# Moving the operands of an encoder's matmuls by 32 bytes, and another order for one stage's loads

## Chip, cores and metric

One core of a Trainium2 chip. The metric is device time of one launch in microseconds, the median of the runs; a profile of one execution goes with it. The engines are named as the profile names them: PE multiplies (PEld is its weight load), DVE and ACT work elementwise, POOL and SP here mostly issue DMAs.

## What is computed

One step of a one-layer encoder on 1024 prompt frames and 64 sample frames (1088 columns in all), width 1024, everything in fp32:

```
proj = rmsnorm(x) @ w_in                      # cb, cc, ch, q, k, v, ga, gb
ya = (cb * causal_conv(cc * ch)) @ w_conv_out
yb = band_attention(q, k, v) @ w_attn_out     # own chunk and 8 chunks before, softmax
x = x + (sigmoid(ga) * ya + sigmoid(gb) * yb) @ w_out
x = x + (silu(h @ w_ff1) * (h @ w_ff3)) @ w_ff2      # h = rmsnorm(x)
return rmsnorm(x), conv states, key and value caches
```

## The kernel before

**Precision.** Every fp32 operand is split into a rounded high part and the rest (`split`, lines 125 to 129: a cast on ACT, a subtraction on DVE). A product is three matmuls: high weights by high data, high weights by the rest of the data, rest of the weights by high data.

**Stages.** In order: norm, transposes and v (lines 443 to 600); the twelve units of the input projection (`run`, matmul at line 263); gates and attention, where PE alternates between gate products (`product`, lines 330 to 332) and attention steps; the two output products ya and yb with the merge (lines 1071 to 1099); `w_out` (wo, lines 1137 to 1142); the up projections of the feed-forward part (22 more units at line 263); the down projection (line 1621).

**A unit.** `run` does a 256 by 256 block of weights by seven products instead of eight. For each of four k it issues six matmuls of 128 rows by 272 columns, always in this order (high weights `wh..`, rest `wl..`; data plane 0 is high, plane 1 is the rest; a half is 272 columns):

| place in the six | weights | data plane, half | data address mod 64 | address of the weights loaded next, mod 64 |
|---|---|---|---|---|
| 1 | high | 0, first | 0 | 0 |
| 2 | high | 0, second | 0 | 0 |
| 3 | high | 1, first | 32 | 0 |
| 4 | high | 1, second | 32 | 32 |
| 5 | rest | 0, first | 0 | 32 |
| 6 | rest | 0, second | 0 | 0 |

"Moving operand" below means the data that is streamed, "weights" the operand that PEld loads; the weights of the next matmul are loaded while the present one streams. The addresses come from the built program. They follow from three things: tiles on the right side of SBUF (pools `apool`, `mspool`, `ws`, allocated downwards from byte 229344) all begin at 32 modulo 64; an operand's planes are rows of HT+8 = 552 floats of which the first 8 are skipped (`operand`, from line 135); high weights skip 8 floats, the rest none (`pair`, from line 142). Tiles on the left side (`t1_pool`, `tpool`, `uo`) begin at 0 modulo 64 unless something small stands ahead of them: `lead1` (line 354) and `lead` (line 1105), 8 floats each, bring `t1_pool` and `tpool` to 32, `uo` has none. The shifts at line 344 place the weights of ya and yb by hand.

**The down projection** takes its weights as moving operand (`ring_of`) and `ht` tiles as weights, both at 32 modulo 64.

**The stage that the second half of the change touches.** Gate products are the entries of `GATES`; before the last three (`LAST`) the attention pools are closed and `uo` is opened in their place with `u` (operand of ya: four pieces `u_d[k]`, 128 x 2 x 1088) and `ob` (operand of yb). Attention's output `o_d` and the reciprocals of its sums `rc_d` are loaded piece by piece, multiplied (line 1060, DVE) and split into `ob` (ACT, then DVE). `gates_in` loads stored gate values, `ga` in four tiles, `gb` in one. ya multiplies by sigmoid(ga), applied in place by ACT (line 1080); DVE then takes the product out of PSUM (line 1083). PE has five PSUM buffers there (`psum2`), so it runs at most five products ahead of DVE. All these loads stand in SP's queue, and SP waits before each load for the one eight places ahead of it: eight of its loads are in flight at most. DVE and ACT work strictly in the order in which their instructions stand.

Of the kernel before, what the change touches and what calls it, by code (L numbers as in the profile page):

```python
# [8 lines left out]
F32 = mybir.dt.float32  # L9
F32R = mybir.dt.float32r  # L10
# [5 lines left out]
P = 128  # L16
# [16 lines left out]
HT = T // 2  # L33
# [5 lines left out]
ROW, STEP = HT + 8, 144  # L39
# [27 lines left out]
def encoder_kernel(ctx: ExitStack, tc: tile.TileContext, ins, outs):  # L67
    nc = tc.nc
# [6 lines left out]

    const = ctx.enter_context(tc.tile_pool(name="const", bufs=1, reuse_waits="tile"))
    dr = ctx.enter_context(tc.tile_pool(name="dr", bufs=1, space=DRAM))
    apool = ctx.enter_context(tc.tile_pool(name="apool", bufs=1, reuse_waits="tile", side="right"))
    mspool = ctx.enter_context(tc.tile_pool(name="mspool", bufs=1, reuse_waits="tile", side="right"))
    ws = ctx.enter_context(tc.tile_pool(name="ws", bufs=8, reuse_waits="tile", side="right"))  # L80
# [13 lines left out]
    u_d = dr.tile([4, P, 2, T], F32, name="u_d")  # L94
# [30 lines left out]
    def split(hi, lo, src):  # L125

        a = act.copy(hi, src)  # L127
        b = vec.tensor_tensor(lo, src, hi.bitcast(F32), op=ALU.subtract)  # L128
        return a.ins, b.ins
# [28 lines left out]
    def three_sums(pool, nm):  # L158
        return {p: operand(pool, p, f"{nm}{p}") for p in (6, 7, 5)}
# [157 lines left out]
    def next_w():  # L317
        i = used[0]
        used[0] += 1
        prep(i + 2)  # L320
        return plan[i]
# [19 lines left out]
    for m in range(0, 8, 2):  # L341
        lds = [
            {"src": ins[nm][0][:, m * P : (m + 2) * P], "w": 2 * P, "shift": shift}
            for nm, shift in (("w_conv_out", (56, 24)), ("w_attn_out", (8, 40)))
        ]
        plan += [(ld, 4, j * P) for ld in lds for j in range(2)]

# [3 lines left out]
    t1_stack = ExitStack()  # L351
    ps1 = t1_stack.enter_context(tc.tile_pool(name="ps1", bufs=1, space=PSUM, reuse_waits="tile"))
    t1_pool = t1_stack.enter_context(tc.tile_pool(name="t1_pool", bufs=1, reuse_waits="tile"))
    t1_pool.tile([P, 8], F32, name="lead1")
    t1 = three_sums(t1_pool, "xs")

    scr = t1_pool.tile([P, 10816], F32, name="scr")
# [400 lines left out]
    for n in range(len(units)):  # L758
# [21 lines left out]
        for _ in r:  # L780
            if n < 2 and si in (2 + n, 5 + n):
                i = 2 * n + si // 5
# [24 lines left out]
    def gate(i, cs):  # L807
        g, m = GATES[i]
        dst = ga_d if g == "a" else gb_d
        for c in cs:  # L810
            o, n = PIECES[c]
            ps = pmm.tile([P, 512], F32, tag="mm", name=f"g{i}_{c}")
            product(ps[:, :n], gate_w[i], xn, o, n)
            st = st_pool.tile([P, HN], F32, tag="st", name=f"gst{i}_{c}")
            act.copy(st[:, :n], ps[:, :n])
            nc.gpsimd.dma_start(dst[m * P : (m + 1) * P, o : o + n], st[:, :n])
# [188 lines left out]
    def between():  # L1005
        credit[0] += PER
        while credit[0] >= 1:
            credit[0] -= 1
            next(steps, None)
# [3 lines left out]
    def gates_in(nm, m):  # L1013
        if nm == "gb":
            t = mp.tile([P, T], F32, tag="rc", name=f"gb{m}", bufs=3)
            nc.sync.dma_start(t, gb_d[m * P : (m + 1) * P])
            for o, n in PIECES:
                sg[nm, m, o] = t[:, o : o + n]
            return
        for o, n in PIECES:  # L1020
            t = sg[nm, m, o] = mp.tile([P, HN], F32, tag=nm, name=f"{nm}{m}_{o}", bufs=8)
            nc.sync.dma_start(t, ga_d[m * P : (m + 1) * P, o : o + n])
# [11 lines left out]
    for i in range(4, len(GATES)):  # L1034
        gate_w[i] = next_w()
        if i == len(GATES) - LAST:
            for _ in steps:
                pass
            att_stack.close()
            uo = pg_stack.enter_context(tc.tile_pool(name="uo", bufs=1, reuse_waits="tile"))  # L1040
            u, ob = (
                Acts(
                    uo.tile([P, 2, 4 * T + 8], F32R, name=nm)[:, :, : 4 * T].rearrange("p l (k t) -> p l k t", k=4)
                )
                for nm in ("u", "ob")
            )
            mp = pg_stack.enter_context(tc.tile_pool(name="mgp", bufs=4, reuse_waits="tile"))
            gates_in("ga", 0)
            for k in range(4):
                nc.sync.dma_start(u.t[:, :, k].bitcast(F32), u_d[k])  # L1050
            for k in range(4):
                o = ob.t[:, 0, k].bitcast(F32)
                nc.sync.dma_start(o, o_d[k * P : (k + 1) * P])
                r = mp.tile([P, T], F32, tag="rc", name=f"rc{k}", bufs=3)
                for j in range(2):
                    src = rc_d[2 * k + j]
                    ld = nc.sync.dma_start(
                        r[j * HD : (j + 1) * HD], bass.AP(tensor=src.tensor, offset=src.offset, ap=[[0, HD], [1, T]])
                    )
                vec.tensor_tensor(r, o, r, op=ALU.mult)  # L1060
                split(ob.t[:, 0, k], ob.t[:, 1, k], r)
            with tc.issue_after(ld.ins):
                gates_in("ga", 1)
                gates_in("gb", 0)
        for c in range(4):
            gate(i, (c,))
            between()
# [5 lines left out]
    for m0 in range(0, 8, 2):  # L1073
        for m in (m0, m0 + 1):
# [3 lines left out]
            for o, n in PIECES:  # L1078
                t = sg["ga", m, o]
# [4 lines left out]
        for m in (m0, m0 + 1):  # L1084
# [3 lines left out]
            for o, n in PIECES:  # L1088
                t, z = sg.pop(("ga", m, o)), sg.pop(("gb", m, o))
# [11 lines left out]

    hp0 = ctx.enter_context(tc.tile_pool(name="hp0", bufs=1, reuse_waits="tile"))
    early = ctx.enter_context(tc.tile_pool(name="early", bufs=1, reuse_waits="tile"))
    lead = ctx.enter_context(tc.tile_pool(name="lead", bufs=1, reuse_waits="tile"))
    lead.tile([P, 8], F32, name="lead")
    tpool = ctx.enter_context(tc.tile_pool(name="tpool", bufs=1, reuse_waits="tile"))
    up_stack = ExitStack()
    psA = up_stack.enter_context(tc.tile_pool(name="psA", bufs=2, space=PSUM, reuse_waits="tile"))
# [196 lines left out]
    def hidden_done(p):  # L1305
# [4 lines left out]
        def keep(c, x):  # L1310
            if p == NF // 2 - 1 and c in LATE:
                hq = ring_of(LATE[c])[:, 3072:4096].rearrange("p (i l t) -> p i l t", i=4, l=2)
            else:
                hq = hp.tile([P, 4, 2, P], F32R, tag="hq", name=f"hq{p}_{c}", bufs=3)
            split(hq[:, :, 0], hq[:, :, 1], x[:, :512].rearrange("p (i t) -> p i t", t=P))
            stored[0] = nc.gpsimd.dma_start(h_d[p, c - 1], hq.rearrange("p i l t -> p (i l t)").bitcast(F32)).ins  # L1316
# [45 lines left out]
    ring = {}  # L1362

    def ring_of(p):
        if p not in ring:
            pool = apool if p in (1, 2, 4, 3) else tpool
            ring[p] = pool.tile([P, 8 * ROW], F32R, tag=f"o{p}", name=f"ring{p}")[:, : 8 * HT]
        return ring[p]

    hts, loaded = [], [0]  # L1370
# [1 line left out]
    def h_load(ks, g, p):  # L1372
        ht = []
        for kp in ks:
            t = ws.tile([P, 4 * STEP], F32R, tag=("wh", "wl")[loaded[0] % 2], name=f"ht{kp}_{g}_{p}")
            t = t[:, :512].rearrange("p (i l t) -> p i l t", i=2, l=2)
            loaded[0] += 1
            nc.sync.dma_start(
                t.rearrange("p i l t -> p (i l t)").bitcast(F32), h_d[kp, p - 1, :, g * 512 : (g + 1) * 512]
            )  # L1380
            ht.append(t)
        hts.append(ht)
# [3 lines left out]
    def refill():  # L1386

        while len(hts) < len(loads_h) and held[0] + len(loads_h[len(hts)][0]) <= 16:
            held[0] += len(loads_h[len(hts)][0])
            h_load(*loads_h[len(hts)])  # L1390
# [6 lines left out]
    class Down:  # L1397
# [10 lines left out]
        def new(self, p):  # L1408
            at = self.kp % 4 * 1024
            self.w[p] = ring_of(p)[:, at : at + 1024].rearrange("p (l n) -> p l n", l=2)  # L1410
            return self.w[p][:, 0], self.w[p][:, 1]
# [99 lines left out]
    for n in range(1, len(names)):  # L1511
# [8 lines left out]
        if n in (4, 6):  # L1520
            nm, src = (("k", ck), ("v", cvv))[n // 2 - 2]
# [21 lines left out]
    bufs = {(hp, "hs"): 1, (hp, "snap"): 3, (hp, "sa"): 4, (hp0, "snap"): 1, (hp0, "sa"): 1}  # L1543
    for n, (i, d) in enumerate(order):
        if n < len(homes):
            pool, tag = homes[n]
# [27 lines left out]
    q = 0  # L1574
    for b, ks in enumerate(blocks):
        first, final = b == 0, b == len(blocks) - 1
        nk = blocks[b + 1] if not final else []
        for g in range(2):
# [28 lines left out]
            for si, js in turns:  # L1607
                p, ht = STEPS[si], hts[base + si]
                key = {1: "A", 6: "A", 5: "A", 3: "A", 2: "B", 7: "D", 4: "D"}[p]
                for j in js:  # L1610
                    i = 2 * g + j
                    if (key, j) not in ps:
                        ps[key, j] = psD.tile(
                            [P, 512], F32, tag="A" if key == "A" else "BD", name=f"{key}{b}_{i}",
                            bufs=2 if key == "A" else 4,
                        )
                    t = ps[key, j]
# [11 lines left out]
                    o = acc[i + 4 * h, d]  # L1629
# [78 lines left out]
```

## Time and profile before

| | |
|---|---|
| median of 3 runs | 1492.48 us (1492.09 to 1495.37) |
| profiled execution, its own time | 1494.22 us |
| its span, first to last instruction | 1492.3 us |
| granted TensorE clock | 0.998 |
| PE busy | 1474.8 us, 99% of the span, 10200 matmuls |
| PEld busy | 1384.6 us, 93% |
| DVE, ACT, POOL busy | 981.5, 680.4 and 129.9 us |

The profiled execution's time is 1.9 us more than its span, and 1.74 us more than the median. A matmul's duration in the profile (about 288 ns for 272 columns) is not what it costs: matmuls overlap, and what counts is the time from one start to the next.

### The profile page before, as it was taken

Reading aid. Unit: us, or ns where it says so; the run is one execution under the profiler, and the core shown is the slowest. Engines: PE = TensorE matmul, PEld = TensorE weight load, DVE = VectorE, ACT = ScalarE, POOL = GpSimd, SP = SyncE. Lnnn points to the kernel's source line nnn. Section 1 sums busy time; section 2 is a strip of 40 time slices with the busy share of each in tenths; the row PEclk is TensorE's granted clock in tenths of the full one; section 3 lists DMA queues with packets and bytes.
Section 4 is the critical chain, followed back from the end, with each engine's and each line's share of the span. In section 5 each row is a group of like instructions: output and inputs, shape, how many; then the busy total and the mean of one; then the engine's idle time right before and its main releaser. Section 6 shows DMA issues by size and latency. Waiting matters only on the chain.

```text
span 1492.3 us, 26460 instructions
## 1 busy us (share of the span) xinstructions
PE 1474.8 (99%) x10200; PEld 1384.6 (93%) x10200; DVE 981.5 (66%) x1852; ACT 680.4 (46%) x1398; POOL 129.9 (9%) x238
## 2 busy tenths in 40 slices
PE   9999999999999999999999999999999999999997
PEld 6899999999999999998889999999999999888886
DVE  7975465633777753763489767666666667857576
ACT  7654333434776652631356444444444445412123
POOL 1300010001111121000100111110011111000000
PEclk9999999999999999999999999999999999999999
DMA  8686523178676539633433454433344438777675
GB/s 287 181 271 213 175 87 116 58 211 227 189 190 179 147 109 292 201 125 130 150 113 107 145 179 161 157 134 113 118 160 145 159 133 301 265 236 239 227 261 204
DMA packets 163933, 264.72 MB, mean 177 GB/s; under 512 B 18528, under 2 KB 98592, under 8 KB 163776
## 3 DMA queue, kind: packets, MB, share of 16 engines
q1 hardware_dynamic: 143024, 196.13, 42.1%
q0 software_dynamic: 19632, 64.81, 12.0%
q10 hardware_dynamic: 1152, 2.10, 0.4%
q8 instruction: 80, 1.31, 0.4%
q14 instruction: 45, 0.37, 0.1%
HBM read 172.89 MB, written 91.92 MB: 177 GB/s over the span
## 4 chain that ended last, share of the span: by engine, by line
PE 89%; DMA 5%; DVE 3%; ACT 1%; SPq 1%; issue 1%; DVEq 0%; ACTq 0%
PE Ab L263 9%; PE Aa L263 9%; PE A L1621 8%; PE Db L263 4%; PE Da L263 4%; PE D L1621 4%; PE Bb L263 2%; PE Ba L263 2%; PE B L1621 2%; PE wo L1138 2%; PE wo L1137 2%; PE wo L1139 2%; PE t L954 2%; PE Ak L263 2%; PE Acb L263 2%; PE Ach L263 2%
## 5 line engine op out<-in xcount | busy, mean ns | idle before, releaser
L1621 PE MATMUL A<-ring,ht 128*128 128x512 f32 x528 | 124.0, 389 | 0.0
L1621 PEld LDWEIGHTS A<-ring,ht 128*128 128x128 f32 x528 | 99.1, 188 | 20.6
L330 PE MATMUL g<-xn,whp 128*128 128x272 f32 x384 | 113.1, 294 | 0.0
L331 PE MATMUL g<-xn,whp 128*128 128x272 f32 x384 | 111.7, 291 | 0.0
L332 PE MATMUL g<-xn,wlp 128*128 128x272 f32 x384 | 110.7, 288 | 0.0
L127 ACT CAST ring<-w2r 128x512 fp32r<-128x512 f32 (+1 forms) x78 | 42.6, 587 | 89.0 <-PE A L1621 50.3
L127 ACT CAST hq<-sa 128x512 fp32r<-128x512 f32 x73 | 45.2, 619 | 81.1 <-DVE sa L1332 55.8
L865 DVE CUSTOM_DVE_ANT_0 p<-s,bb 128x640 f32<-128x640 f32 (+5 forms) x72 | 47.5, 661 | 42.7 <-DMA ga_d<-gst 26.8
L1316 POOL DMA_DIRECT2D h_d<-hq x73 | 38.9, 533 | 408.7 <-DVE hq L128 218.1
L330 PEld LDWEIGHTS g<-xn,whp 128*128 128x128 f32 x384 | 72.3, 188 | 1.0
L332 PEld LDWEIGHTS g<-xn,wlp 128*128 128x128 f32 x384 | 72.4, 189 | 0.5
L331 PEld LDWEIGHTS g<-xn,whp 128*128 128x128 f32 x384 | 72.4, 188 | 0.3
L128 DVE TENSOR_TENSOR hq<-sa,hq 128x512 fp32r<-128x512 f32 x73 | 50.3, 690 | 30.1 <-ACT hq L127 29.9
L128 DVE TENSOR_TENSOR wla<-rawa,wha 128x512 fp32r<-128x512 f32 x56 | 38.4, 688 | 40.1 <-ACT wha L127 40.1
L1621 PE MATMUL D<-ring,ht 128*128 128x512 f32 x264 | 62.6, 389 | 0.0
L263 PE MATMUL Aa<-tt,wha 128*128 128x272 f32 x352 | 58.6, 288 | 0.8 <-ACT sa_Q L251 0.8
L1621 PEld LDWEIGHTS D<-ring,ht 128*128 128x128 f32 x264 | 49.6, 188 | 10.3
L263 PE MATMUL Aa<-mg,wha 128*128 128x272 f32 x352 | 58.6, 288 | 0.4 <-DVE sa L1297 0.4
L263 PE MATMUL Ab<-mg,whb 128*128 128x272 f32 x352 | 58.8, 288 | 0.0
L263 PE MATMUL Ab<-tt,whb 128*128 128x272 f32 x352 | 58.6, 288 | 0.0
L127 ACT CAST wha<-rawa 128x512 fp32r<-128x512 f32 x56 | 34.6, 620 | 52.0 <-PE Ab L263 35.5
L128 DVE TENSOR_TENSOR ring<-w2r,ring 128x512 fp32r<-128x512 f32 (+1 forms) x78 | 48.6, 645 | 11.5 <-ACT ring L127 11.5
(537 smaller groups left out, 4380.0 us busy)
## 6 DMA issues: line engine op xcount, KB each, us to landing
ht<-h_d SPq DMA_DIRECT2D x154, 256.0 KB, 3.7
h_d<-hq POOLq DMA_DIRECT2D x73, 512.0 KB, 3.4
rawa<-in_w_ff SPq DMA_DIRECT2D x11, 1024.0 KB, 5.7
rawb<-in_w_ff SPq DMA_DIRECT2D x11, 1024.0 KB, 5.3
w2r<-in_w_ff SPq DMA_DIRECT2D x11, 1024.0 KB, 7.3
qd<-q_d SPq DMA_DIRECT2D x32, 272.0 KB, 4.6
rawp<-in_w_in SPq DMA_DIRECT2D x6, 1024.0 KB, 7.0
u_d<-scr SPq DMA_DIRECT2D x8, 544.0 KB, 4.9
```

The costliest lines, as they stand in the source:

```text
L127: a = act.copy(hi, src)
L128: b = vec.tensor_tensor(lo, src, hi.bitcast(F32), op=ALU.subtract)
L263: newest[0] = mm(t[:, j, :HN], w[:, k, :], x[p][:, k, l, j * HN : (j + 1) * HN], start=p in (1, 2, 7) and k == 0 and n == 0, stop=k == 3 a ...
L330: mm(out, a, first, start=k == 0, stop=False)
L331: mm(out, a, then, start=False, stop=False)
L332: mm(out, b, p, start=False, stop=k == kt - 1)
L865: vec.tensor_tensor_reduce(out=s if len(ps.shape) == 2 else s.rearrange("p (a b) -> p a b", a=2), in0=ps, in1=bias if len(ps.shape) == 2 e ...
L954: nc.tensor.transpose(tp[:, i * P : (i + 1) * P], s[:, i * P : (i + 1) * P], ident)
L1137: mm(ps, x(k, 0), wh, start=f, stop=False)
L1138: mm(ps, x(k, 0), wl, start=False, stop=False)
L1316: stored[0] = nc.gpsimd.dma_start(h_d[p, c - 1], hq.rearrange("p i l t -> p (i l t)").bitcast(F32)).ins
L1621: mm(t, ht[k][:, j, x], w[:, l], start=p in (1, 2, 7) and k == 0 and n == 0, stop=k == len(ks) - 1 and n == 2, skip_group_check=p in (6, 5 ...
```

## The change

Part one moves addresses. A small tile `edge` (8 floats) is put at the right end of SBUF, so that everything on the right side moves 32 bytes down; `lead1` and `lead` go, so that `t1_pool` and `tpool` move with it; `uo` gets a `lead`, and the shifts of ya's and yb's weights are set anew, so that these move 32 bytes up modulo 64 together. Distances between a moving operand and the weights beside it stay, modulo 256. `ring` and `ht`, the down projection's operands, are cut 8 floats later, which puts them where they were. In the table above every 0 becomes 32 and every 32 becomes 0. Attention's operands stay.

Part two changes the order of loads. `u`'s pieces 0 and 1 stay ahead of attention's pieces 0 and 1, pieces 2 and 3 go behind the third; the four tiles of the first `ga` go from the front to behind all of them.

```diff
+    edge = ctx.enter_context(tc.tile_pool(name="edge", bufs=1, reuse_waits="tile", side="right"))
+    edge.tile([P, 8], F32, name="edge")
     apool = ctx.enter_context(tc.tile_pool(name="apool", bufs=1, reuse_waits="tile", side="right"))
...
-            for nm, shift in (("w_conv_out", (56, 24)), ("w_attn_out", (8, 40)))
+            for nm, shift in (("w_conv_out", (8, 40)), ("w_attn_out", (24, 56)))
...
-    t1_pool.tile([P, 8], F32, name="lead1")
...
+            uo.tile([P, 8], F32, name="lead")
...
-            gates_in("ga", 0)
             for k in range(4):
-                nc.sync.dma_start(u.t[:, :, k].bitcast(F32), u_d[k])
-            for k in range(4):
+                for q in {0: (0,), 1: (1,), 2: (), 3: (2, 3)}[k]:
+                    nc.sync.dma_start(u.t[:, :, q].bitcast(F32), u_d[q])
                 o = ob.t[:, 0, k].bitcast(F32)
...
             with tc.issue_after(ld.ins):
+                gates_in("ga", 0)
                 gates_in("ga", 1)
...
-    lead = ctx.enter_context(tc.tile_pool(name="lead", bufs=1, reuse_waits="tile"))
-    lead.tile([P, 8], F32, name="lead")
...
-            ring[p] = pool.tile([P, 8 * ROW], F32R, tag=f"o{p}", name=f"ring{p}")[:, : 8 * HT]
+            ring[p] = pool.tile([P, 8 * ROW], F32R, tag=f"o{p}", name=f"ring{p}")[:, 8 : 8 + 8 * HT]
...
-            t = t[:, :512].rearrange("p (i l t) -> p i l t", i=2, l=2)
+            t = t[:, 8:520].rearrange("p (i l t) -> p i l t", i=2, l=2)
```

On PE the order is the same, instruction for instruction. It differs on SP, DVE and ACT, in this stage alone (lines of the changed kernel are one or two higher). First SP's queue from the end of attention on, before:

```order
L890 DMA o_d<-co_s 64x32 x2
L1022 DMA ga_0_6566<-ga_d 128x272
L1022 DMA ga_272_6568<-ga_d 128x272
L1022 DMA ga_544_6570<-ga_d 128x272
L1022 DMA ga_816_6572<-ga_d 128x272
L1050 DMA u<-u_d 128x2x1088 x4
L1053 DMA ob<-o_d 128x1088
L1057 DMA rc_6579<-rc_d 64x1088 x2
L1053 DMA ob<-o_d 128x1088
L1057 DMA rc_6586<-rc_d 64x1088 x2
```

The same place in SP's queue of the changed kernel:

```order
L891 DMA o_d<-co_s 64x32 x2
L1052 DMA u<-u_d 128x2x1088
L1054 DMA ob<-o_d 128x1088
L1058 DMA rc_6572<-rc_d 64x1088 x2
L1052 DMA u<-u_d 128x2x1088
L1054 DMA ob<-o_d 128x1088
L1058 DMA rc_6580<-rc_d 64x1088 x2
L1054 DMA ob<-o_d 128x1088
L1058 DMA rc_6587<-rc_d 64x1088 x2
L1052 DMA u<-u_d 128x2x1088 x2
L1054 DMA ob<-o_d 128x1088
L1058 DMA rc_6596<-rc_d 64x1088 x2
```

All four pieces of `u` stood ahead of attention's first piece; now two of them stand behind nine loads of attention's pieces, and the tiles of `ga` follow at the end. On DVE, where ya's products begin to be taken out of PSUM (`ga<-ya`), before:

```order
L1060 TENSOR_TENSOR rc_6586<-ob,rc_6586 128x1088
L128 TENSOR_TENSOR ob<-rc_6586,ob 128x1088
L1083 TENSOR_TENSOR ga_0_6566<-ya_0_6979,ga_0_6566 128x272
L1060 TENSOR_TENSOR rc_6593<-ob,rc_6593 128x1088
L1083 TENSOR_TENSOR ga_272_6568<-ya_272_6994,ga_272_6568 128x272
L1083 TENSOR_TENSOR ga_544_6570<-ya_544_7009,ga_544_6570 128x272
L128 TENSOR_TENSOR ob<-rc_6593,ob 128x1088
L1083 TENSOR_TENSOR ga_816_6572<-ya_816_7024,ga_816_6572 128x272
L1060 TENSOR_TENSOR rc_6600<-ob,rc_6600 128x1088
```

And in the changed kernel:

```order
L1061 TENSOR_TENSOR rc_6580<-ob,rc_6580 128x1088
L130 TENSOR_TENSOR ob<-rc_6580,ob 128x1088
L1061 TENSOR_TENSOR rc_6587<-ob,rc_6587 128x1088
L130 TENSOR_TENSOR ob<-rc_6587,ob 128x1088
L1061 TENSOR_TENSOR rc_6596<-ob,rc_6596 128x1088
L1085 TENSOR_TENSOR ga_0_6602<-ya_0_6983,ga_0_6602 128x272
L130 TENSOR_TENSOR ob<-rc_6596,ob 128x1088
L1085 TENSOR_TENSOR ga_272_6604<-ya_272_6998,ga_272_6604 128x272
```

The first three pieces of attention now stand ahead of ya's first product, and the last piece's split (`ob<-rc_6596`) behind it. On ACT, the sigmoids of the first `ga` stood well ahead of this place before; in the changed kernel they stand here, with the table load, and the last cast for `ob` behind the first of them:

```order
L816 COPY gst_3_6967<-g_3_6942 128x272
L1082 ACT_TABLE_LOAD
L1082 ACTIVATE ga_0_6602<-ga_0_6602 128x272
L129 CAST ob<-rc_6596 128x1088
L1082 ACTIVATE ga_272_6604<-ga_272_6604 128x272
L1082 ACTIVATE ga_544_6606<-ga_544_6606 128x272
L1082 ACTIVATE ga_816_6608<-ga_816_6608 128x272
```

So the last quarter of `ob` now waits, on an engine that works in order, for the landing of a load that is issued after its own.

## The prediction

> **What bounds the kernel now.** The page first: busy times and the chain of work that ended last.
>
> ```profile
> PE 1474.8 (99%) x10200; PEld 1384.6 (93%) x10200; DVE 981.5 (66%) x1852; ACT 680.4 (46%) x1398; POOL 129.9 (9%) x238
> PE 89%; DMA 5%; DVE 3%; ACT 1%; SPq 1%; issue 1%; DVEq 0%; ACTq 0%
> ```
>
> PE sets the end: the chain lies on it for 89%. So two things can move the time, the start-to-start time of a matmul and the few places where PE waits. For the first, a stretch of 100 us in the up projections, and the same stage as a sequence (first row of the table of windows, then PE's timeline):
>
> ```profile
> 820.00:920.00 100.00, 100.00 (x797) 100.00 (x796) 70.33 (x119) 44.03 (x86) 11.42 (x22) 1.00 0.43 152
> ...
> 900.41 0.67 PE L263 MATMUL Ab<-tt,whb 128*128 128x272 f32 x4
> 900.91 0.41 PE L263 MATMUL Ab<-tt,wlb 128*128 128x272 f32 x2
> 901.17 0.67 PE L263 MATMUL Ab<-tt,whb 128*128 128x272 f32 x4
> 901.67 0.41 PE L263 MATMUL Ab<-tt,wlb 128*128 128x272 f32 x2
> ```
>
> 797 matmuls in 100 us are 125.5 ns each, at a granted clock of 1.00; four with high weights and two with the rest take 0.755 us together. By the start times of all 952 such sixes of line 263, of which these rows are two, the places 1 to 6 of the table in the section on the kernel take 127.6, 127.4, 125.0, 124.0, 125.1 and 125.8 ns. Within a place the figure is the same to a few tenths for every tile, every unit and both halves of the kernel, so it depends on addresses alone and on their lowest bits. The grouped rows say the same more coarsely:
>
> ```profile
> L263 PE MATMUL Aa<-mg,wha 128*128 128x272 f32 x352 | 58.6, 288 | 0.4 <-DVE sa L1297 0.4
> L263 PE MATMUL Aa<-mg,wla 128*128 128x272 f32 x176 | 36.3, 288 | 0.0
> ```
>
> 88 runs of four in 58.6 us are 666 ns a run, which is three starts and one duration: less a last duration of 285, 127 ns for each of places 1 to 3. 88 runs of two in 36.3 us are 412.5 ns, less 288, 124.5 for place 5.
>
> **Part one, addresses.** Distances stay, and so does PE's order; what changes is that 0 and 32 modulo 64 change places. Places 4 and 6 are the nearest pair that the trace has: in both the distance between data and next weights is 0 modulo 256, both are the last with their weights, and they differ in the phase, 32 at place 4 (124.0) and 0 at place 6 (125.8). I read 1.8 ns as the price of both operands at 0 instead of 32. Places 1, 2 and 6 then gain 1.8 each, place 4 loses 1.8, places 3 and 5 (125.0 and 125.1, one operand at 0 and one at 32) exchange roles and stay. That is -3.6 ns for a six, and 952 sixes give **-3.4 us**.
>
> The other products, with their rows:
>
> ```profile
> L330 PE MATMUL g<-xn,whp 128*128 128x272 f32 x384 | 113.1, 294 | 0.0
> L331 PE MATMUL g<-xn,whp 128*128 128x272 f32 x384 | 111.7, 291 | 0.0
> L330 PE MATMUL ya<-u,whp 128*128 128x272 f32 x128 | 36.9, 288 | 0.8 <-DVE ga L1083 0.8
> L331 PE MATMUL ya<-u,whp 128*128 128x272 f32 x128 | 36.9, 289 | 0.0
> L1138 PE MATMUL wo<-wlo,mg 128*128 128x512 f32 x128 | 50.4, 393 | 0.0
> L1139 PE MATMUL wo<-who,mg 128*128 128x512 f32 x128 | 50.1, 391 | 0.0
> L514 PE MATMUL pvv<-whv,xn 128*128 128x512 f32 x64 | 25.8, 403 | 0.1
> L1621 PE MATMUL A<-ring,ht 128*128 128x512 f32 x528 | 124.0, 389 | 0.0
> ```
>
> Gates (1152 matmuls, two lines of three shown): three of six at 0 and 0, one at 32 and 32, so -3.6 x 192 = -0.7 us. ya and yb (768): two of three at 0 and 0, none at 32 and 32, so 512 x 1.8 = -0.9. wo and v (128 and 64 triples): two at 0, one at 32, -0.35. The down projection keeps its addresses: 0. Sum of part one **-5.4 us**. The bounds: if the price is that between the classes, 126.9 (mean of places 1, 2 and 6) against 124.0, thus 2.9 ns, the same counts give -8.7 us. If the phase is nothing, 0. Below that, the sign could be the other, +5.4: ya's second matmul has its data at 32 and takes 289 in its row where the first, at 0 and 0, takes 288, so it isn't everywhere that 32 looks cheaper. I take 1.8, since places 4 and 6 are the nearest rows.
>
> [...]
>
> **Part two, loads.** Where PE waits: all waits of 550 to 610 us, PE's rows at the two places, and DVE's rows there.
>
> ```profile
> PE yb L331 <- DVE ob L128: 0.9, 1, 0.9
> PE ya L330 <- DVE ga L1083: 0.8, 1, 0.8
> PE yb L330 <- ACT ob L127: 0.5, 1, 0.5
> ...
> 589.78 0.29 PE L332 MATMUL ya<-u,wlp 128*128 128x272 f32 x1
> 590.84 0.39 PE L330 MATMUL ya<-u,whp 128*128 128x272 f32 x1 [0.77 <-DVE ga L1083]
> ...
> 593.94 0.29 PE L330 MATMUL yb<-ob,whp 128*128 128x272 f32 x1
> ...
> 597.30 0.30 PE L332 MATMUL yb<-ob,wlp 128*128 128x272 f32 x1
> ...
> 577.83 1.29 DVE L1060 TENSOR_TENSOR rc<-ob,rc 128x1088 f32<-128x1088 f32 x1 [7.57 <-DMA rc<-rc_d]
> 583.65 1.29 DVE L1060 TENSOR_TENSOR rc<-ob,rc 128x1088 f32<-128x1088 f32 x1 [2.08 <-DMA rc<-rc_d]
> 589.14 1.29 DVE L1060 TENSOR_TENSOR rc<-ob,rc 128x1088 f32<-128x1088 f32 x1 [1.39 <-DMA rc<-rc_d]
> 593.26 1.29 DVE L1060 TENSOR_TENSOR rc<-ob,rc 128x1088 f32<-128x1088 f32 x1
> ```
>
> PE loses 1.06 - 0.13 = 0.9 us at 589.8 and, since yb's first eleven matmuls should take 1.38 us and take 3.36, 2.0 us before 597.3: **3.0 us** in all with the slow matmul after the first wait. What is late is the last pieces of attention: the pairs (`o_d`, `rc_d`) land 5.5 us apart, DVE's rows show it (577.8, 583.65, 589.1). Until then DMA is full:
>
> ```profile
> 560.00:565.00 5.00, 5.00 (x42) 5.00 (x42) 0.00 (x0) 0.77 (x2) 1.08 (x2) 1.00 1.02 416
> 580.00:585.00 5.00, 5.00 (x42) 5.00 (x41) 2.58 (x2) 0.56 (x3) 0.54 (x1) 1.00 1.02 262
> ...
> L1050 SPq DMA_DIRECT2D u<-u_d x4: 580/608/870, 552.4 to 554.3; - x4
> ...
> DMA to landing us min/median/max: 8.5/12.4/17.1
> ```
>
> The DMA share (last but one) is 1.02 in both windows, 416 GB/s while `u` moves and 262 while pairs do. `u`'s first piece lands 8.5 us after 552.4, at 560.9, its last 17.1 after 554.3, at 571.4: 3.5 us a piece. The queue is a line of fixed length, so a new order moves who is late.
>
> Without `ga` ahead (half a pair's bytes, some 2 us; SP's first issue is 550.3), `u` 0 lands at an estimated 556.8. Behind it, by 5.7 us a pair and 3.5 a piece: pair 0 at 562.5, `u` 1 at 566.0, pairs 1 and 2 at 571.7 and 577.4, `u` 2 at 580.9, `u` 3 at **584.4**, pair 3 at 590.0, `ga`'s first tile at 590.5. ya starts at 580.9 and needs `u` 3 nine matmuls later, at 582.0:
>
> ```profile
> L330 PE MATMUL ya<-u,whp x128: 282/288/394, 580.9 to 667.7; 128*128 128x272 f32 x128
> ...
> 552.45 1.28 ACT L1080 ACT_TABLE_LOAD   x1 [1.08 <-DMA ga<-ga_d]
> 553.75 0.43 ACT L1080 ACTIVATE ga<-ga 128x272 f32<-128x272 f32 x1
> 587.32 0.43 DVE L1083 TENSOR_TENSOR ga<-ya,ga 128x272 f32<-128x272 f32 x1
> 590.47 1.10 ACT L127 CAST ob<-rc 128x1088 fp32r<-128x1088 f32 x1 [4.10 <-DVE rc L1060]
> ```
>
> So the old wait goes and two others come. ya's first product waits 2.4 us for `u`, ends at 584.8, the fifth at 590.8 (1.51 each). The sixth needs a buffer back: `ga` at 590.5, table load 1.28, sigmoid 0.43, DVE 0.43, thus 592.7, a wait of 1.9. The cast of the last `ob` (1.10) stands ahead of the second sigmoid and its split (1.29 on DVE) ahead of the second product, so that comes at 595.0, 0.8 later than PE wants it. yb starts at 598.0, with `ob` complete at 594.6. Before, yb ran as if it had started at 597.3 - 1.4 = 595.9: **+2.1 us**. If the mixture of both kinds of loads moves faster than the kinds one after the other and `u` 3 is there at 582, everything behind is 2.4 earlier: -0.3. The best case takes all 3.0 us away; the worst, `u` 3 as late as pair 2's old landing, 589.1 minus 2, costs 2.7 more than the middle: +4.8. I take **+1.0**, near the middle of -0.3 and +2.1. What stands behind ya on ACT in the old order, the earlier sigmoids, was hidden under gate products; that cover is gone, and the 1.9 above is its price.
>
> **Sum.** 1494.22 (the profiled execution) - 5.4 + 1.0 = 1489.8. The median of the runs is 1.74 below that execution, so the median after is **1488.1 us**. Faster or slower means by over 0.2%, 3.0 us, about what a measurement of this kernel can tell from no change: below 1489.5 or above 1495.5.
>
> **Rivals.**
> 1. *The move does nothing*: start-to-start times follow distances alone, which are kept. For it: place 1 and place 6 have the same distance and phase and differ by 1.8 too, so what comes before and after counts. [...] Then only the loads remain: 1492.5 + 1.0 = 1493.5.
> 2. *The phase is worth the whole difference between the classes*, and the loads take the old waits away: -8.7 - 3.0, 1480.8. For it: both places with both operands at 32 that the trace has with distance 0 (place 4, and gates' second matmul) take 124.0 to 124.2, and none at 0 and 0 in line 263 is below 125.4.
> 3. *The phase has the other sign*, the slower side: a row of 1088 bytes is 17 blocks of 64; begun at 32 it touches 18. If the stream is fetched so, four of six matmuls touch one block more after the change and two one less, before it is the reverse. Its price, taken as large as my term: +5.4, with the loads 1492.5 + 6.4 = 1498.9. It decides if places 1, 2 and 6 rise. Against it: the two places with data at 32 are the cheapest two of the six.
> 4. *`u` 3 is later than 587*: the loads cost +4.8 or more and eat the gain: 1492.5 - 5.4 + 4.8 = 1491.9, and above 1495.5 if part one is below 2 us.
>
> **Chances.** Forecast 0.46 (faster 0.40, the same 0.06); rival 1: 0.12 (same 0.09, slower 0.03); rival 2: 0.18, faster; rival 3: 0.16, slower; rival 4: 0.08 (same 0.04, slower 0.04). Together faster 0.58, same 0.19, slower 0.23. The forecast's own range is 1484 to 1491. For 8 in 10 the range takes rivals 1 and 4 in, the upper part of rival 2 and the lower of rival 3: 1480 to 1498.
>
> **What would show it.** In line 263 places 1, 2 and 6 near 125.8, 125.6 and 124.0, place 4 near 125.8; a window of 100 us in the up projections with 801 matmuls for 797. In the merge, a wait of ya's first product for `u`, and of the sixth for `ga` L1085 on DVE; none of yb for `ob`. The down projection unchanged. It is wrong if place 4 keeps 124.0 while places 1 and 2 keep 127.5 (rival 1), or if yb still waits for `ob`.

## The result and the profile after

| | before | after |
|---|---|---|
| median of the runs compared | 1493.89 us (1492.09 to 1497.51, 12 runs) | 1492.26 us (1491.19 to 1494.90, 12 runs) |
| ratio after to before | | 0.999, 95% interval 0.9981 to 0.9999 |
| profiled execution: time, span | 1494.22, 1492.3 us | 1494.23, 1492.4 us |
| granted clock | 0.998 | 0.999 |

The change is within 0.2% of no change: a tenth of a per cent faster, with an interval that nearly reaches 1. The forecast was 1488.1, with 1484 to 1491 as its own range; the time lies above that range and nearest to the first rival (1493.5, the move does nothing). The wide range, 1480 to 1498, holds it because it takes rivals in, and that the median came out on the faster side is luck: the term that was to make it faster turned out to be nothing. The sum went wrong on that term, its largest.

The page of after, busy times and chain:

```profile
PE 1473.8 (99%) x10200; PEld 1384.8 (93%) x10200; DVE 983.0 (66%) x1852; ACT 680.5 (46%) x1398; POOL 130.0 (9%) x238
PE 57%; issue 35%; POOL 3%; DMA 2%; DVE 2%; ACT 1%; SPq 0%; POOLq 0%; ACTq 0%; DVEq 0%
```

PE is as busy as before to 1 us in 1474.8. The chain gives 35% to "issue" where before it gave PE 89%. No stage moved by more than 1.8 us with it (table of stages below), so the split between PE and "issue" is how the chain was followed back, and no time.

The up projections, the stretch of 100 us on which the prediction rests, then one six of PE's timeline with the first four of the next, and the grouped rows:

```profile
820.00:920.00 100.00, 100.00 (x797) 100.00 (x797) 70.60 (x120) 43.82 (x84) 11.95 (x23) 1.00 0.45 158
```

```profile
899.48 0.67 PE L265 MATMUL Ab<-tt,whb 128*128 128x272 f32 x4
899.98 0.41 PE L265 MATMUL Ab<-tt,wlb 128*128 128x272 f32 x2
900.23 0.67 PE L265 MATMUL Db<-tt,whb 128*128 128x272 f32 x4
```

```profile
L265 PE MATMUL Aa<-mg,wha 128*128 128x272 f32 x352 | 58.7, 288 | 0.4 <-DVE sa L1297 0.4
...
L265 PE MATMUL Aa<-mg,wla 128*128 128x272 f32 x176 | 36.3, 288 | 0.0
```

797 matmuls again, not 801; a six takes 0.75 us; 58.7 and 36.3 where before had 58.6 and 36.3. Place by place, from the start times of all 952 sixes (intervals with a wait in them left out), in ns:

| | 1 | 2 | 3 | 4 | 5 | 6 | sum |
|---|---|---|---|---|---|---|---|
| before | 127.51 | 127.31 | 125.10 | 124.04 | 125.13 | 125.79 | 754.90 |
| after | 127.60 | 127.21 | 125.16 | 124.01 | 125.24 | 125.66 | 754.89 |

Every operand of these six moved from 0 to 32 modulo 64 or back, and no place moved by more than 0.13 ns. That is what "wrong if" named: place 4 keeps 124.0 while places 1 and 2 keep 127.5.

The merge, first PE's waits from 545 to 612 us, then PE, DVE and ACT where they arise:

```profile
PE ya L332 <- DVE ga L1085: 1.0, 2, 0.6
```

```profile
580.36 0.29 PE L332 MATMUL ya<-u,whp 128*128 128x272 f32 x1
...
587.75 0.28 PE L334 MATMUL ya<-u,wlp 128*128 128x272 f32 x1
588.61 0.40 PE L332 MATMUL ya<-u,whp 128*128 128x272 f32 x1 [0.57 <-DVE ga L1085]
```

```profile
585.97 1.29 DVE L1061 TENSOR_TENSOR rc<-ob,rc 128x1088 f32<-128x1088 f32 x1 [8.35 <-DMA ga<-ga_d]
588.11 0.44 DVE L1085 TENSOR_TENSOR ga<-ya,ga 128x272 f32<-128x272 f32 x1 [0.85 <-ACT ga L1082]
589.10 1.29 DVE L130 TENSOR_TENSOR ob<-rc,ob 128x1088 fp32r<-128x1088 f32 x1 [0.55 <-ACT ob L129]
```

```profile
586.36 1.28 ACT L1082 ACT_TABLE_LOAD   x1 [5.36 <-DMA ga<-ga_d]
587.65 0.43 ACT L1082 ACTIVATE ga<-ga 128x272 f32<-128x272 f32 x1
587.99 1.08 ACT L129 CAST ob<-rc 128x1088 fp32r<-128x1088 f32 x1
```

From `ga` on the chain is the predicted one: `ga` lands late, at 586.3, table load and sigmoid follow it, DVE takes the first product out of PSUM at 588.11, and PE's sixth product, ready at 587.88, begins at 588.61. A second wait stands behind the split of the last `ob` at 589.10. (DVE's first row names `ga` as what ended its wait, but that product reads `rc` and began before `ga` landed; the last pair landed at 585.9.) No wait of yb for `ob` is left. With the slower matmul behind each wait PE loses 1.5 us here, against 3.0 in the profile of before.

Why the last piece of `u` came early enough: the loads of `u` in the trace of after, and the DMA's share and GB/s (last two columns) while they and the pairs move.

```profile
L1052 SPq DMA_DIRECT2D u<-u_d x4: 542/562/587, 549.4 to 563.7; - x4
...
DMA to landing us min/median/max: 5.6/13.5/16.1
```

```profile
560.00:565.00 5.00, 5.00 (x42) 5.00 (x42) 2.28 (x2) 1.44 (x2) 1.08 (x2) 1.00 1.03 362
580.00:585.00 5.00, 5.00 (x42) 5.00 (x41) 0.00 (x0) 0.39 (x1) 0.54 (x1) 1.00 1.09 234
```

The queue is full as before (shares of 1.03 and 1.09, before 1.02 in both windows); the last piece is issued at 563.7 and lands 16.1 us later, at 579.8, where 584.4 was worked out. ya begins at 580.4 and waits for none.

Yet the spans are 1492.3 and 1492.4 us. Against before, after is 1.5 us shorter in norm and v, 1.0 longer in units, gates and attention, 1.5 shorter at ya and yb, 0.3 longer in wo and 1.8 in the up projections. PE's waits from 900 to 1240 us, where before has none:

```profile
PE Aa L265 <- ACT sa_Q L253: 1.1, 1, 1.1
```

With its neighbours this is 1.3 us at 967; 0.3 more is lost at 1094. It is no mark of the new addresses: of the experiments below, `loads_only` and `u_only`, with the old ones, lose 1.2 and 1.0 us at the same place. Nor is it one of the new loads: `gap24` and `gap48`, with the old order, lose 0.9 and 0.6 there, `after_gap16`, with the new one, loses nothing, and `addr_only`, with the old one, loses 1.5 at 818. Such waits come and go from profile to profile; what sets them off stays open.

### The profile page after: what moved, and what is told of

It reads as the page before. It is cut to its first block, busy times and chain, and to the rows that moved or that the text cites. A ratio compares the mean times of both kernels' runs of the same rounds, so it can differ in the third digit from the quotient of the medians.

```text
span 1492.4 us, 26462 instructions
## 1 busy us (share of the span) xinstructions
PE 1473.8 (99%) x10200; PEld 1384.8 (93%) x10200; DVE 983.0 (66%) x1852; ACT 680.5 (46%) x1398; POOL 130.0 (9%) x238
## 4 chain that ended last, share of the span: by engine, by line
PE 57%; issue 35%; POOL 3%; DMA 2%; DVE 2%; ACT 1%; SPq 0%; POOLq 0%; ACTq 0%; DVEq 0%
PE A L1621 8%; PE D L1621 4%; PE Ab L265 3%; PE Aa L265 3%; PE B L1621 2%; PE t L955 2%; PE g L332 2%; PE g L333 2%; PE Aq L265 2%; PE Db L265 2%; PE Acb L265 2%; PE Ach L265 2%; PE Acc L265 2%; PE g L334 2%; PE pv L980 2%
## 5 line engine op out<-in xcount | busy, mean ns | idle before, releaser
L1621 PE MATMUL A<-ring,ht 128*128 128x512 f32 x528 | 124.0, 390 | 0.0
L265 PE MATMUL Aa<-mg,wha 128*128 128x272 f32 x352 | 58.7, 288 | 0.4 <-DVE sa L1297 0.4
L265 PE MATMUL Ab<-tt,whb 128*128 128x272 f32 x352 | 58.7, 288 | 0.0
```

What stands on the lines that cost most here:

```text
L265: newest[0] = mm(t[:, j, :HN], w[:, k, :], x[p][:, k, l, j * HN : (j + 1) * HN], start=p in (1, 2, 7) and k == 0 and n == 0, stop=k == 3 a ...
L1621: mm(t, ht[k][:, j, x], w[:, l], start=p in (1, 2, 7) and k == 0 and n == 0, stop=k == len(ks) - 1 and n == 2, skip_group_check=p in (6, 5 ...
```

## The experiments

Theory at this point: the phase modulo 64 is worth nothing, start-to-start times are set by how the operands stand to each other, and the order of loads changes the merge by less than executions differ. Its rivals: the addresses gained a little and the loads lost it, or the reverse; or the six is bound by something that addresses don't touch at all.

**The two halves apart.** `addr_only` has the new addresses with the old loads:

```diff
+    edge.tile([P, 8], F32, name="edge")
-    t1_pool.tile([P, 8], F32, name="lead1")
...
+            uo.tile([P, 8], F32, name="lead")
-    lead.tile([P, 8], F32, name="lead")
...
-            for nm, shift in (("w_conv_out", (56, 24)), ("w_attn_out", (8, 40)))
+            for nm, shift in (("w_conv_out", (8, 40)), ("w_attn_out", (24, 56)))
```

> Part one alone: all addresses of the change, loads in the old order. Theory D (start-to-start times follow the distances between operands modulo 256, the phase modulo 64 is worth nothing): places 1 to 6 of the six as before within 0.2 ns, the three waits of ya and yb back at 3.0 us, ratio to before 1.000. Theory P (32 modulo 64 is cheaper by 1.8 ns, and something else of the change hid it): places 1, 2 and 6 lower by 1 to 2 ns, ratio 0.996 to 0.997. Theory S (part one has a small gain of its own that a place by place reading misses): ratio 0.999.

`loads_only` has the old addresses with the new loads:

```diff
-            gates_in("ga", 0)
-            for k in range(4):
-                nc.sync.dma_start(u.t[:, :, k].bitcast(F32), u_d[k])
...
+                for q in {0: (0,), 1: (1,), 2: (), 3: (2, 3)}[k]:
+                    nc.sync.dma_start(u.t[:, :, q].bitcast(F32), u_d[q])
...
+                gates_in("ga", 0)
```

> Part two alone: the new order of loads at the old addresses. Theory D: the whole of the difference is here: two waits of ya for DVE, 1.3 to 1.5 us together with the slow matmul behind each, none of yb; 1.5 us less than before, ratio 0.999. Theory S: nothing or half of it, ratio 0.9995 to 1.000.

Measured: `addr_only` 1492.82 us, ratio 0.9995 (0.9986 to 1.0003); `loads_only` 1494.44 us, ratio 1.0004 (0.9996 to 1.0013). Neither half differs from before, so no gain of one hides a loss of the other beyond these intervals. The six takes 754.88 and 754.87 ns. In the same 100 us, `addr_only` and then `loads_only`:

```profile
820.00:920.00 100.00, 100.00 (x797) 100.00 (x797) 70.75 (x120) 44.67 (x86) 11.76 (x22) 1.00 0.44 156
```

```profile
820.00:920.00 100.00, 100.00 (x797) 100.00 (x797) 70.72 (x120) 44.52 (x86) 11.75 (x22) 1.00 0.44 156
```

In the merge, `loads_only` shows the wait for `ga`, 0.4 us, and `addr_only`, with the old loads, shows no wait at all, where before lost 3.0. So theory D was right on the places, and wrong on the waits of both kernels: the 3.0 us did not come back in `addr_only`, and `loads_only` is not 1.5 us faster.

**The loads taken apart.** `ga_only` moves only the first `ga` behind the pairs; `u_only` moves only the pieces of `u` between them, with `ga` still ahead.

```diff
-            gates_in("ga", 0)
...
+                gates_in("ga", 0)
```

> Only the first ga goes behind the pairs, the four pieces of u stay together ahead of them. If the gain comes from mixing the two kinds of loads: pairs still land 5.5 us apart, the last ob is ready at best 2 us earlier, the sigmoids wait for ga until 592 or later, PE's waits 3 to 5 us, time +0 to +2 us. If it comes from taking ga out of the front: waits about 1.5 us, time -1.5 us.

```diff
-                nc.sync.dma_start(u.t[:, :, k].bitcast(F32), u_d[k])
...
+                for q in {0: (0,), 1: (1,), 2: (), 3: (2, 3)}[k]:
+                    nc.sync.dma_start(u.t[:, :, q].bitcast(F32), u_d[q])
```

> Only the pieces of u are mixed with the pairs, ga stays in front. If the gain comes from mixing: u's last piece lands at 581 to 583, the last pair at 587 to 588, no wait for ga's first products, PE's waits 0 to 1.5 us, time -1.5 to -3 us, thus better than the change. If it comes from taking ga out of the front: pairs land as late as before and u later, waits 3 us or more, time 0 or above.

Measured: `ga_only` 1492.67 us, ratio 1.0 (0.9991 to 1.0009). `u_only` 1494.24 us, ratio 1.0015 (1.0003 to 1.0026): slower by less than 0.2%, though the interval leaves 1 out. PE's waits in the merge, `ga_only`, then `u_only`:

```profile
PE ya L330 <- DVE ga L1083: 0.7, 1, 0.7
```

```profile
PE ya L330 <- DMA u<-u_d: 1.7, 1, 1.7
```

Both waits of the prediction exist, each in the kernel that isolates it. The wait for `u` was seen only with `ga` still in front. The loads of `u` in `u_only`:

```profile
L1051 SPq DMA_DIRECT2D u<-u_d x4: 543/566/1153, 554.4 to 572.1; - x4
...
DMA to landing us min/median/max: 8.8/15.2/15.8
```

Its last piece lands 15.8 us after its issue at 572.1, at 588.0; in after, without `ga` ahead, it lands at 579.8 and nothing waits for it. Of the expectations, neither reading for `ga_only` came out (PE loses 0.9 us there, and the time is that of before); for `u_only` the second came nearer, with 2.1 us lost, wait and slow matmuls together.

**Why the pairs land 5.5 us apart.** `rc_rows` reads 64 different rows of attention's output where the program reads one row of reciprocals 64 times; its merge so works on other data than the reference's.

```diff
-                        r[j * HD : (j + 1) * HD], bass.AP(tensor=src.tensor, offset=src.offset, ap=[[0, HD], [1, T]])
+                        r[j * HD : (j + 1) * HD], o_d[k * P + j * HD : k * P + (j + 1) * HD]
```

> The kernel before, but the loads of reciprocals read 64 rows of attention's output each instead of 64 times one row, same bytes, so the merge's data are not the reference's. If reading one row again and again is what makes the pairs slower than pieces of u: pairs land 3.0 to 4.0 us apart, DMA near 400 GB/s throughout, the waits of yb are gone. If not: pairs stay 4.5 to 5.7 us apart.

One run: 1491.27 us, span 1489.3. DVE's products of its pairs (start times):

```profile
575.16 1.29 DVE L1060 TENSOR_TENSOR rc<-ob,rc 128x1088 f32<-128x1088 f32 x1 [6.19 <-DMA rc<-o_d]
580.30 1.29 DVE L1060 TENSOR_TENSOR rc<-ob,rc 128x1088 f32<-128x1088 f32 x1 [1.38 <-DMA rc<-o_d]
585.08 1.29 DVE L1060 TENSOR_TENSOR rc<-ob,rc 128x1088 f32<-128x1088 f32 x1 [0.68 <-DMA rc<-o_d]
```

The same rows of `gap16` (below), whose loads are those of before, with one row read 64 times:

```profile
574.32 1.29 DVE L1062 TENSOR_TENSOR rc<-ob,rc 128x1088 f32<-128x1088 f32 x1 [5.80 <-DMA rc<-rc_d]
579.08 1.29 DVE L1062 TENSOR_TENSOR rc<-ob,rc 128x1088 f32<-128x1088 f32 x1 [1.00 <-DMA rc<-rc_d]
583.55 1.29 DVE L1062 TENSOR_TENSOR rc<-ob,rc 128x1088 f32<-128x1088 f32 x1 [0.37 <-DMA rc<-rc_d]
```

5.1 and 4.8 us apart with different rows, 4.8 and 4.5 with the repeated one: reading one row over and over is not what makes the pairs slow. What does stays open. Their spacing differs between profiles of the same order of loads, from 4.5 (`gap16`) to 5.8 us (before), and so does what PE loses in the merge:

| PE's loss in ya and yb, us | |
|---|---|
| old order of loads, nine profiles | 3.0 (before), 2.4, 1.3, 0.5, 0.2, 0, 0, 0, 0: mean 0.8 |
| new order, three profiles | 1.5 (after), 0.7, 0.6: mean 0.9 |

**Distances.** The six does depend on addresses if the distance moves. A tile `gap` between the pools `mspool` and `ws` lowers the weights alone; `ht`, which lives in `ws`, is cut later so that the down projection keeps its distance. The loads are those of before. With 8, 16 and 32 floats:

```diff
+    gap = ctx.enter_context(tc.tile_pool(name="gap", bufs=1, reuse_waits="tile", side="right"))
+    gap.tile([P, 16], F32, name="gap")
...
-            t = t[:, :512].rearrange("p (i l t) -> p i l t", i=2, l=2)
+            t = t[:, 16:528].rearrange("p (i l t) -> p i l t", i=2, l=2)
```

> The kernel before with the weights' pool alone 32 bytes lower: the distance from data to weights is 32 less modulo 256 in every product but the down projection, the data stay where they were. Theory D (distances decide): the six changes place by place; places 1, 4 and 6 come to distance 224, which takes 125 where it is seen now (place 5), so place 1 falls to about 125 and place 4 rises to about 125; the sum of the six moves by 1 to 5 ns from 754.9, in either direction, 1 to 5 us of the whole. Rival N (the order of the six and which weights are loaded again decide, not addresses): every place as before, sum 754.9, ratio 1.000.

> The same with 64 bytes. Theory D: places 1, 4 and 6 come to distance 192, where place 2 takes 127.3, so places 4 and 6 rise by 1 to 3 ns; sum of the six 756 to 762, up to 7 us slower. Rival N: as before.

> The same with 128 bytes. Theory D: places 1, 4 and 6 at distance 128, place 2 at 64, place 3 at 224, place 5 at 96; by ya's matmuls, the only ones that show 128 and 64 (126.4 and 123.9), places 4 and 6 rise and place 2 falls; sum within 3 ns of 754.9. Rival N: as before.

Measured: `gap8` 1493.16 us, ratio 0.9993 (0.9982 to 1.0004). `gap16` **1487.47 us**, ratio 0.9958 (0.9943 to 0.9973). `gap32` 1496.39 us, ratio 1.0016 (1.0007 to 1.0026). The expectation for `gap16` had the wrong sign. The 100 us and the groups of `gap16`:

```profile
820.00:920.00 100.00, 100.00 (x804) 100.00 (x803) 70.47 (x120) 45.39 (x87) 13.26 (x25) 1.00 0.48 170
```

```profile
L265 PE MATMUL Aa<-mg,wha 128*128 128x272 f32 x352 | 58.3, 287 | 0.5 <-DVE sa L1299 0.5
...
L265 PE MATMUL Aa<-mg,wla 128*128 128x272 f32 x176 | 36.2, 288 | 0.0
```

The same groups of `gap32`:

```profile
L265 PE MATMUL Aa<-mg,wha 128*128 128x272 f32 x352 | 58.9, 289 | 0.4 <-DVE sa L1299 0.4
L265 PE MATMUL Aa<-mg,wla 128*128 128x272 f32 x176 | 36.6, 288 | 0.0
```

804 matmuls for 797, and both groups shorter at 64 bytes, both longer at 128. The expectations for `gap8` and `gap32` held in part: `gap8`'s six moved by 3.3 ns, within 1 to 5, but its place 4 fell where it was to rise; `gap32`'s moved by 3.2, just beyond the 3 that were given. Four more kernels narrow down what this is. `after_gap16` puts the same gap into the changed kernel, so that every operand has the other phase at `gap16`'s distances:

```diff
+    gap.tile([P, 16], F32, name="gap")
...
-            t = t[:, 8:520].rearrange("p (i l t) -> p i l t", i=2, l=2)
+            t = t[:, 24:536].rearrange("p (i l t) -> p i l t", i=2, l=2)
```

> The changed kernel with the same 64 bytes taken out of the distance between data and weights as in gap16 (a tile of 16 floats between the pools mspool and ws; ht cut later, so that the down projection keeps its distance). Theory A, distance decides and the phase modulo 64 is nothing at any distance: the six places take what they took in gap16, 126.5, 125.05, 121.0, 126.6, 124.2 and 125.0, sum 748.5 ns, and the span is 1485 us give or take 1.5 for the loads. Rival B, the phase mattered and was masked only at the old distances: places 1, 2 and 6 against 4 move by 1 to 3 ns from gap16's, the sum leaves 748.5 by more than 1 ns, 1 us or more in the span. Rival C, the new order of loads is a loss where PE is faster ahead of it: sum 748.5, but the stage of ya and yb 1.5 us or more above gap16's 99.8.

`gap16_lo8` is `gap16` with the rest weights alone 32 bytes on:

```diff
-        return hi[:, :, 8 : 8 + P], lo[:, :, :P]
+        return hi[:, :, 8 : 8 + P], lo[:, :, 8 : 8 + P]
```

> gap16 with only the rest weights of each pair 8 floats further right (as the high ones stand), so that the distance changes at places 4 (192 to 224) and 5 (160 to 192) alone; the four others keep theirs. Theory A, each place's time follows the distance from its own data to the next weights: places 4 and 5 go to what gap8 showed at these distances, 123.75 and 123.9, the others stay at 126.5, 125.05, 121.0 and 125.0: sum 745.3 ns, 3.0 us less than gap16, span 1482. Rival B, the time follows the pattern of all operands together (a place's neighbours count): the other four places move by over 0.5 ns, and the sum may come out anywhere between 745 and 752, span 1482 to 1488.

`gap24` and `gap48` are `gap16` with another size (`gap.tile([P, 24]` and `gap.tile([P, 48]`):

> The gap at 24 floats, 96 bytes less distance modulo 256 than before. Theory A, the distance decides with no simple slope: places 1, 4 and 6 at 160, 2 at 96, 3 at 0, 5 at 128. The one reading that is at hand for place 2 or 5 near there (160: 125.3 and 124.2; 96 at place 5: 128.0) gives no forecast below a width: a sum between 745 and 758 ns, middle 752, span 1482 to 1495. Rival, a slope of -0.1 ns a byte goes on: 745.2 ns, span 1482.

> The gap at 48 floats, 192 bytes less distance. Places 1, 4 and 6 at 64, 2 at 0, 3 at 160, 5 at 32. Theory A, the distance counts modulo 256 and by place: a sum between 745 and 760 ns; place 2 at 0 between 124 and 127.5, which places 1, 4 and 6 showed there. Rival, only the amount of room between data and weights counts, more gap being worse beyond 64 bytes: above 758.1 ns, span above 1495.

Measured: `after_gap16` 1488.35 us, ratio 0.9974 (0.9963 to 0.9986); `gap16_lo8` 1486.99, ratio 0.9965 (0.9952 to 0.9977); `gap24` 1492.96 and `gap48` 1494.65, one run each (before, beside all four: 1491.91). The 100 us of `after_gap16`:

```profile
820.00:920.00 100.00, 100.00 (x804) 100.00 (x803) 70.19 (x119) 45.38 (x87) 13.39 (x25) 1.00 0.49 173
```

The places of all of them, in ns as above. From the data to the weights loaded next, before has 0, 192, 96, 0, 224 and 0 bytes modulo 256 at places 1 to 6; each gap of n floats takes 4n bytes off every distance, modulo 256:

| bytes off the distance | 1 | 2 | 3 | 4 | 5 | 6 | sum |
|---|---|---|---|---|---|---|---|
| 0 (before) | 127.51 | 127.31 | 125.10 | 124.04 | 125.13 | 125.79 | 754.90 |
| 32 (`gap8`) | 126.33 | 125.26 | 126.96 | 123.75 | 123.89 | 125.46 | 751.65 |
| 64 (`gap16`) | 126.51 | 125.05 | 121.04 | 126.61 | 124.24 | 125.02 | 748.46 |
| 64, other phase (`after_gap16`) | 126.53 | 125.04 | 120.99 | 126.62 | 124.23 | 125.01 | 748.42 |
| 64, rest weights 32 (`gap16_lo8`) | 126.54 | 125.09 | 121.08 | 125.84 | 124.99 | 125.03 | 748.56 |
| 96 (`gap24`) | 126.80 | 126.11 | 123.91 | 126.08 | 123.96 | 125.82 | 752.69 |
| 128 (`gap32`) | 127.47 | 126.83 | 124.24 | 125.77 | 128.02 | 125.81 | 758.13 |
| 192 (`gap48`) | 125.17 | 126.68 | 129.85 | 124.86 | 123.43 | 124.75 | 754.75 |

What follows. Phase is nothing at a second distance too: `gap16` and `after_gap16` agree at every place to 0.05 ns, while the same places differ from before by up to 4.1. Distance is worth -6.4 to +3.2 ns of a six, with no slope that goes on (96 turns back) and no rule that more room is worse (192 is as good as 0). It is the distance and not the weights' own address: `gap8` and after both bring the weights down by 32 bytes; place 3 goes from 125.10 to 126.96 in `gap8`, where the data stay, and is 125.16 in after, where they go along. Moving both by 64 bytes or more was not tried, nor a gap of 256 bytes, which would show whether the pattern repeats. The theory that a place's time follows the distance from its own data to the next weights fell: in `gap16_lo8` place 4 was to fall to 123.75 and place 5 to 123.9, and they are 125.84 and 124.99. Only those two moved, by -0.77 and +0.75, and their sum stayed (250.85 and 250.83 ns): the start of the fifth matmul moved, the sixth started where it had. Its rival, that the other four places move too, fell as well.

By stages (us; the column of ya and yb takes in 3.7 us of wo, its sample rows), the 64 bytes and the two phases:

| | norm, v | units | gates, attention | ya, yb | wo | up | down |
|---|---|---|---|---|---|---|---|
| before | 66.28 | 258.88 | 252.77 | 102.92 | 98.38 | 470.06 | 231.73 |
| after | 64.80 | 259.45 | 253.18 | 101.42 | 98.69 | 471.84 | 231.72 |
| `gap16` | 65.44 | 257.78 | 252.94 | 99.76 | 99.19 | 466.88 | 231.75 |
| `after_gap16` | 65.08 | 257.45 | 252.58 | 100.31 | 99.41 | 466.16 | 231.73 |

6.4 ns on 952 sixes are 6.1 us. In units and up projections 4.3 us of it arrive with `gap16` and 5.3 with `after_gap16`: the rest goes into longer gaps between matmuls at waits and changes of product in these stages, 1.8 and 0.8 us more of them than in the profile of before. Almost all of the gain is in the sixes: with `gap16` a gate product's matmul takes 125.5 ns where before has 125.3, one of ya or yb 125.0 where it has 125.2 and 125.3, and one of wo, with its 512 columns, 230.5 where it has 228.8. `gap16` is faster than both kernels of this study. `after_gap16` has the new loads and `gap16_lo8` the other distance of the rest weights on top of it, and neither is faster than it beyond the intervals.

## Where the prediction was right and where wrong, step by step

- **PE sets the end.** Right: 99% busy before and after, and `gap16` shows that less time per matmul shortens the span (748.46 ns for a six where before has 754.90, a span of 1485.0 us where before has 1492.3).
- **Within a place the figure "depends on addresses alone and on their lowest bits".** Right on the addresses as far as the gaps show: moving the weights changes every place, by up to 4.8 ns (place 3, 125.10 before and 129.85 in `gap48`). The lowest bits of each address by themselves are not it, as the next step shows.
- **"I read 1.8 ns as the price of both operands at 0 instead of 32", from places 4 and 6.** This is the step that failed. The two places differ in phase, but also in what runs before them and after them, and the comparison gave all of the difference to the phase. With the phases exchanged, place 4 takes 124.01 and place 6 125.66: the 1.7 ns belong to the places. The price measured is 0.0, and with it the term for the sixes (-3.4 us predicted, -0.01 ns x 952 measured). The smaller terms go too: a gate product's matmul takes 125.27 before and 125.45 after, ya's 125.17 and 125.06, yb's 125.31 and 125.30. Of the -5.4 us of part one nothing is left, and `addr_only` says the same in time: 0.9995 (0.9986 to 1.0003). Rival 1 had the sign that pointed this way: places 1 and 6 stand at the same distance and the same phase and differ by 1.7, so a difference between places needs no phase.
- **Rivals 2 and 3**, a larger price and the other sign: both fell with the same rows.
- **The down projection unchanged.** Right: 231.73 and 231.72 us.
- **PE loses 3.0 us at ya and yb.** True of the profiled execution, but nothing to count on: it is the largest loss of nine profiles of that order of loads (of nine kernels, one each), four of which lose nothing. As a base for the sum it was a sample of one.
- **The loads, +1.0 us.** The mechanism was right in part, the size was not. Links that were seen: no wait of yb for `ob`; the sixth product waits for `ga` behind table load and sigmoid and the seventh for the last `ob`'s split, 1.5 us together where 1.9 and 0.8 were worked out. Link that was not: ya's first product waiting for `u`. `u`'s last piece was put at 584.4 and landed at 579.8; the first piece was 1.8 us early (555.0 instead of 556.8), then the three pairs ahead of it took 5.0 to 5.5 us instead of 5.7 and the pieces of `u` 2.7 to 3.4 instead of 3.5. `ga` landed at 586.3 instead of 590.5 for the same reason. Against the profile of before the stage changed by -1.5 us, while the mean loss of the new order's profiles is 0.1 above that of the old order's: the runs do not tell the two orders apart. Rival 4 did not come about in after; `u_only`, where `u` 3 lands at 588.0, shows its mechanism, at 1.7 us of waiting.
- **The sum.** With 0 for part one and what the means of the profiles give for the loads, nothing is left, and nothing is what the runs of both halves show. Not settled: whether the 0.1% of the ratio is real, since neither half alone shows it.

## What to carry to other kernels

The price of a property has to come from the same place with and without it; two places that differ in the property differ in more, and a second pair, alike in the property and still different (here places 1 and 6, 127.51 and 125.79 ns), tells at once how much more. A loss behind a DMA that lands just in time is a sample (here 0 to 3.0 us in nine profiles of one order of loads): before it is counted as something to win, look whether another execution has it. Where PE is the bound and each matmul loads new weights (here 10200 loads for 10200 matmuls), a small tile that moves only the weights tries another distance at little cost. A few sizes have to be tried, since the sign can't be read from the neighbours (64 bytes took 6.4 ns off a six, 128 added 3.2), and the whole kernel has to be measured, since other products may lose by it (wo's matmul went from 228.8 to 230.5 ns in `gap16`).

## What had not been expected of the hardware

- The distance between streamed data and weights is worth from -0.42% to +0.16% of this kernel in 64 and 128 bytes, with single places between 120.99 and 129.85 ns for the same 272 columns. For the 64 bytes a six of 756 to 762 ns had been expected, and it took 748.46; what it is that the distance disturbs stays open.
- Moving data and weights together by 32 bytes is worth nothing at either of two distances (754.90 and 754.89; 748.46 and 748.42 ns).
- Moving the rest weights alone shifted one start by 0.77 ns and left the six as it was (748.46 and 748.56 ns), while moving high and rest weights together changed it by 3.2 to 5.4 ns for each 32 bytes up to 128. That suggests that the high weights decide, but they were not moved alone, so it is not shown.
